# A hybrid attention and recurrence layer: other orders round the fourth head pair, a fifth buffer for raw FFN weights, another cut of the last row

## The chip, the cores and the metric

The kernel runs on one core of one Trainium2 chip. The metric is the device time of one execution in microseconds (us); lower is better. The engines are PE (TensorE), DVE (VectorE), ACT (ScalarE), POOL (GpSimd) and SP (SyncE, which here only starts transfers).

## The reference

One decoder layer over 16 meta tokens and 1024 tokens of width 1024, all in float32:

```python
u = rmsnorm(h, g_pre_mix)
q, k, v, xr, yr = split(u @ w_in)               # 512, 128, 128, 512, 512 columns
attn = sliding_window_attention(q, k, v, sinks) # 8 heads of 64, 2 kv heads, window 128
xr = causal_depthwise_conv(xr, conv_w, conv_b)  # 4 taps
hr = rg_lru(xr, w_a, b_a, w_x, b_x, lam)        # gates, then a scan along the tokens
rec = gelu(yr) * hr
h = h + rmsnorm(concat([attn, rec]) @ w_out, g_post_mix)
h = h + rmsnorm(square(relu(rmsnorm(h, g_pre_ffn) @ w_ff1)) @ w_ff2, g_post_ffn)
```

The attention sees a window of 128 keys, and each head has a sink that takes part in the softmax. The meta tokens are dropped from the output.

## The kernel before, in words

Every float32 operand of a product is split into a high and a low part. ACT writes the high (lines 96 and 117) and DVE the low (lines 99 and 118). `mm3` (lines 125, 128 and 129) issues three matmuls for a product: high by high, high by low, low by high. `behind(name, ...)` lets an instruction stand after another one in the schedule, without a semaphore of its own. The rest of the order comes from a scheduler that works through the program by priorities and by the buffers of the pools.

PSUM has four pools of two banks each: `acc`, `s`, `pt` and `o`. SBUF has pools of rotating buffers by tag, among them `raw` (2 buffers, weights as they come from memory), `e` (2), `d` (4) and `ws` (4, split weights).

The stages, in order of time:

1. Norm, transposition, and the projections to k, v, the first q and the first x.
2. Attention in four head pairs (`j` from 0 to 3). A pair has two halves, and a half two block pairs. For each block pair PE makes scores (lines 592 to 600), DVE adds the mask and takes the row maximum (line 616), ACT takes the exponential (line 82), POOL adds the sums of the parts (line 632), DVE divides (line 633), PE transposes (line 644), ACT and DVE split, POOL masks the diagonals (line 648), and PE multiplies with the values (`av`, line 658). ACT and DVE take the result out (lines 671 and 672). Between these PE has the projections of the later q and x blocks and of y0 to y3 as filling, each in pieces of 256 to 512 columns that use the two `acc` banks in turn. A q piece leaves its bank by `split_scaled`, two highs and two lows; an x piece by an ACT copy (line 460); a y piece by a DVE copy (line 715).
3. The gates of the recurrence (line 800): matmuls that use 64 of the 128 rows, in groups between the pieces of y1 to y3. Then decay, square root and scan on ACT and DVE.
4. The product with `w_out`, its norm, and the first FFN product.
5. The second FFN product as seven block products (`PLAN`), each in eight steps. `fetch_2` loads a step's raw weights three steps ahead, `prep_2` combines two raw blocks where the product needs their sum or difference (`combine`, line 1022) and splits them, `step_mm` multiplies. The raw weights alternate between the two `raw` and the two `e` buffers.
6. The rows of the output: `finish_late` adds the last block product, squares, scales, takes the root, and writes each row of 128 tokens in two halves, one from the SP queue and one from the ACT queue (lines 1418 and 1421). The last row of tokens has its last product in two parts of 256 columns.

The tiles that the change touches: `km` and `vm` hold the keys and values of the meta tokens, `mask` the window's mask. In the kernel before they are three constant tiles, which hold their space to the end.

Of the kernel before, what the change touches and what calls it, by code (L numbers as in the profile page):

```python
# [9 lines left out]
F32 = mybir.dt.float32  # L10
# [27 lines left out]
def hybrid_layer(  # L38
# [15 lines left out]

    bufs = {"raw": 2, "ws": 4, "a": 16, "b": 17, "c": 8, "d": 4, "e": 2}
    uid = [0]
# [200 lines left out]
    def project(w, pieces, sink, begun=None):  # L257
        wh, wl = w
        for t0, n in pieces:
            acc = bank("acc")  # L260
            for kc in range(KC):
                uh, ul = u[kc]
                ins = mm3(
                    acc[:, :n], (wh[:, kc, :], wl[:, kc, :]),
                    (uh[:, t0 : t0 + n], ul[:, t0 : t0 + n]),
                    kc == 0, kc == KC - 1,
                )
                if kc == 1 and begun is not None:
                    begun.append(ins)
            sink(acc[:, :n], t0, n)  # L270
# [167 lines left out]
    def sink_v(acc, t0, n):  # L438
        if t0 == 0:
            nc.scalar.copy(vmt[:, META], acc[:, 0:NMETA])  # L440
        nc.scalar.copy(vt[:, t0 : t0 + n], acc)

    def new_q():
# [65 lines left out]
    for c in range(NLRU):  # L509
# [6 lines left out]

    mask = const.tile([P, 256], F32, name="mask")
    nc.gpsimd.memset(mask, 0.0)
    nc.gpsimd.affine_select(
        out=mask[:, 0:P], in_=mask[:, 0:P], pattern=[[1, P]], compare_op=ALU.is_gt,  # L520
        fill=NEG, base=0, channel_multiplier=-1,
    )
    nc.gpsimd.affine_select(
        out=mask[:, P:256], in_=mask[:, P:256], pattern=[[-1, P]],
        compare_op=ALU.is_ge, fill=NEG, base=0, channel_multiplier=1,
# [53 lines left out]
    def scores(j, half, q):  # L579

        g, pairs = j // 2, []
        for bp in range(2):
# [8 lines left out]
            for h in range(2):  # L591
# [21 lines left out]
                for i in range(2):  # L613
# [23 lines left out]
    def attend(j, half, pairs):  # L637
        g = j // 2
        o_ = slot("e", [P, 512])
        for bp, sn in enumerate(pairs):  # L640
# [15 lines left out]
            def av(v, oc, n, pc, first, last):  # L656
                for k, m in enumerate((mhv, mlv)):
                    nc.tensor.matmul(  # L658
                        po[:, :, oc : oc + n], v, m[:, :, pc : pc + n],
                        start=first and k == 0, stop=last and k == 1,  # L660
                        skip_group_check=True,
                    )

# [46 lines left out]
    def fill_y(c):  # L710
        def run(w):
            y = slot("b" if c == 1 else "d", [P, T])

            def sink(acc, t0, n):
                nc.vector.tensor_copy(y[:, t0 - NMETA : t0 - NMETA + n], acc)

            begun[c] = []
            project(w, REAL2, sink, begun[c])
            ys[c] = y
# [69 lines left out]
    def gates(c):  # L789
# [3 lines left out]
        for t0, n in ((0, 348), (348, 348), (696, 344)):  # L793
# [498 lines left out]
    ]  # L1292

    def fetch_2(n):
        i, q = steps[n]
        if i == 6:
            r = slot(("raw", "e")[n % 2], [P, 2, 512])
            nc.sync.dma_start(r, w2_sum[q])
            return [r]
        wx = PLAN[i][1]  # L1300
        tags = (("raw", "e"), ("e", "raw"))[n % 2]
        raws = []
        for (a, b), tag in zip(wx[:2], tags):
# [34 lines left out]
    for n, p in enumerate(third):  # L1338
# [3 lines left out]
        if n + 2 < 16:  # L1342
            raw_c[third[n + 2]] = fetch_c(third[n + 2])
        if n >= 13:
            raw_2[n - 13] = fetch_2(n - 13)
        if n + 1 < 16:
# [53 lines left out]
    def finish_late(j, y, parts):  # L1400
# [15 lines left out]
        nc.vector.reciprocal(rs, root)  # L1416
        for c, eng in zip(COLS[::-1], (nc.sync, nc.scalar)):
            held.append(nc.vector.scalar_tensor_tensor(
# [105 lines left out]
```

## Time and profile before

| | |
|---|---|
| median of 3 runs | 955.91 us (955.73 to 956.14) |
| profiled execution, its own time | 955.25 us |
| its span | 953.5 us |
| PE busy | 942.0 us, 99% |
| DVE busy | 682.4 us, 72% |
| ACT busy | 498.3 us, 52% |
| POOL busy | 152.7 us, 16% |
| transfers | 140.76 MB, 148 GB/s over the span |

The 1.75 us between the span and the execution's own time lie outside what the profile's rows show. The chain that ended last runs for 88% of the span on PE, for 7% on DVE and for 2% on ACT. A row of the timeline gives start, duration, engine, line, operation, output and inputs; what stands in brackets at its end is the time that the engine stood idle ahead of it, and what released it. Matmuls overlap, so the pace of PE is read from start to start: about 0.23 us for 512 columns and 0.12 us for 256.

### The profile page before, as it was taken

What the parts mean: (1) busy time and instruction counts of PE and PEld (TensorE: products, weight loads), DVE (VectorE), ACT (ScalarE), POOL (GpSimd) and SP (SyncE); (2) the same over time, 40 slices, a digit from 0 to 9 for tenths busy, and PEclk for the clock granted to TensorE, in tenths of its full rate; (3) what the DMA queues carried; (4) which work ended last, traced back from release to release, by engine and by line L of the source; (5) the groups of instructions that cost most, each with busy time, mean ns of one, the idle gap of its engine ahead of it and who ended that gap; (6) DMA issues with size and microseconds to landing.
All of it is one profiled execution on the core that took longest, in us unless ns stands there. A gap on an engine that the chain in (4) does not pass through costs nothing.

```text
span 953.5 us, 12448 instructions
## 1 busy us (share of the span) xinstructions
PE 942.0 (99%) x4677; PEld 785.7 (82%) x4677; DVE 682.4 (72%) x968; ACT 498.3 (52%) x822; POOL 152.7 (16%) x196
## 2 busy tenths in 40 slices
PE   9999999999999999999999999999999999999997
PEld 8999998878788877888888878888888888888886
DVE  6679999777966886665755566567567676779884
ACT  7556676468355564443655565664433343445451
POOL 2115666500021100000111001100111100003020
PEclk9999999999999999999999999999999999999999
DMA  8121101203145457485646457644678865656422
GB/s 293 49 56 34 45 2 34 67 17 117 42 166 192 153 181 238 158 284 177 218 160 216 157 177 217 226 153 109 171 179 188 208 218 185 185 190 155 116 84 89
DMA packets 85629, 140.76 MB, mean 148 GB/s; under 512 B 5785, under 2 KB 48937, under 8 KB 85569
## 3 DMA queue, kind: packets, MB, share of 16 engines
q1 hardware_dynamic: 75104, 108.51, 36.1%
q0 software_dynamic: 9600, 29.36, 11.7%
q10 hardware_dynamic: 864, 2.10, 0.6%
q8 instruction: 37, 0.61, 0.3%
q14 instruction: 24, 0.19, 0.1%
HBM read 115.70 MB, written 23.07 MB: 146 GB/s over the span
## 4 chain that ended last, share of the span: by engine, by line
PE 88%; DVE 7%; ACT 2%; issue 1%; DMA 1%; POOL 1%; DVEq 0%; SPq 0%; ACTq 0%; POOLq 0%
PE ps_acc L125 10%; PE ps_acc L128 10%; PE ps_acc L129 10%; PE ps_pt L128 6%; PE ps_pt L129 6%; PE ps_pt L125 6%; PE ps_s L125 6%; PE ps_s L129 6%; PE ps_s L128 6%; PE ps_o L125 5%; PE ps_o L128 5%; PE ps_o L129 5%; DVE c L852 1%; PE ps_o L658 1%; PE ps_o L996 1%
## 5 line engine op out<-in xcount | busy, mean ns | idle before, releaser
L96 ACT CAST ws<-raw 128x1024 fp32r<-128x1024 f32 (+1 forms) x70 | 71.8, 1025 | 118.9 <-PE ps_o L128 45.8
L99 DVE TENSOR_TENSOR ws<-raw,ws 128x1024 fp32r<-128x1024 f32 (+1 forms) x71 | 85.4, 1203 | 45.5 <-ACT ws L96 45.5
L125 PE MATMUL ps_acc<-a,ws 128*128 128x256 f32 (+2 forms) x256 | 85.5, 334 | 1.1 <-ACT d L460 1.0
L129 PE MATMUL ps_acc<-a,ws 128*128 128x256 f32 (+2 forms) x256 | 85.0, 333 | 0.0
L128 PE MATMUL ps_acc<-a,ws 128*128 128x256 f32 (+2 forms) x256 | 85.0, 332 | 0.0
L99 DVE TENSOR_TENSOR b<-b,b 128x1024 fp32r<-128x1024 f32 (+2 forms) x48 | 57.6, 1199 | 25.5 <-PE ps_o L128 19.8
L96 ACT CAST ws<-e 128x1024 fp32r<-128x1024 f32 x42 | 44.0, 1047 | 57.0 <-PE ps_o L128 31.4
L96 ACT CAST b<-b 128x1024 fp32r<-128x1024 f32 (+2 forms) x48 | 49.5, 1030 | 38.8 <-DVE b L1022 36.4
L99 DVE TENSOR_TENSOR ws<-e,ws 128x1024 fp32r<-128x1024 f32 x42 | 51.3, 1222 | 20.0 <-ACT ws L96 20.0
L648 POOL TENSOR_SCALAR_AFFINE_SELECT c<-c 128x512 fp32r<-128x512 f32 x64 | 55.8, 893 | 26.8 <-ACT c L96 20.6
L125 PEld LDWEIGHTS ps_acc<-a,ws 128*128 128x128 f32 x256 | 48.2, 188 | 6.4 <-ACT d L460 1.2
L129 PEld LDWEIGHTS ps_acc<-a,ws 128*128 128x128 f32 x256 | 48.2, 188 | 5.1 <-issue 0.2
L178 POOL TENSOR_TENSOR rs<-ms,half_pow 128x1 f32<-128x1 f32 x26 | 19.3, 749 | 205.9 <-DVE ms L174 204.7
L128 PEld LDWEIGHTS ps_acc<-a,ws 128*128 128x128 f32 x256 | 48.1, 188 | 4.6 <-issue 0.4
L125 PE MATMUL ps_acc<-ws,b 128*128 128x512 f32 (+1 forms) x120 | 46.3, 385 | 0.0
L129 PE MATMUL ps_acc<-ws,b 128*128 128x512 f32 (+1 forms) x120 | 46.2, 385 | 0.0
L128 PE MATMUL ps_acc<-ws,b 128*128 128x512 f32 (+1 forms) x120 | 46.1, 384 | 0.0
L125 PE MATMUL ps_pt<-ws,b 128*128 128x512 f32 x112 | 44.2, 394 | 0.0
L128 PE MATMUL ps_pt<-ws,b 128*128 128x512 f32 x112 | 44.1, 393 | 0.0
L129 PE MATMUL ps_pt<-ws,b 128*128 128x512 f32 x112 | 43.9, 392 | 0.0
L125 PE MATMUL ps_s<-ws,b 128*128 128x512 f32 x110 | 43.4, 395 | 0.0
L129 PE MATMUL ps_s<-ws,b 128*128 128x512 f32 x110 | 43.2, 393 | 0.0
(429 smaller groups left out, 2720.9 us busy)
## 6 DMA issues: line engine op xcount, KB each, us to landing
raw<-in_w_ff_dram SPq DMA_DIRECT2D x58, 512.0 KB, 4.4
e<-in_w_ff_dram SPq DMA_DIRECT2D x42, 512.0 KB, 4.1
raw<-in_w_in_dram SPq DMA_DIRECT2D x12, 512.0 KB, 5.1
d<-in_w_ff_dram SPq DMA_DIRECT2D x12, 512.0 KB, 4.2
s_dram<-d POOLq DMA_DIRECT2D x12, 512.0 KB, 4.4
e<-in_w_ff_dram POOLq DMA_DIRECT2D x10, 512.0 KB, 5.8
raw<-in_w_ff_dram POOLq DMA_DIRECT2D x10, 512.0 KB, 5.8
c<-in_x_dram SPq DMA_DIRECT2D x8, 512.0 KB, 8.9
```

Of the source, the lines that this page charges most:

```text
L96: nc.scalar.copy(hi, src)
L99: low = nc.vector.tensor_tensor(lo, src, f32(hi), op=ALU.subtract).ins
L125: ins = nc.tensor.matmul(dst, lh, rh, start=start, stop=False, skip_group_check=True).ins
L128: nc.tensor.matmul(dst, lh, rl, start=False, stop=False, skip_group_check=True)
L129: last_mm[0] = nc.tensor.matmul(dst, ll, rh, start=False, stop=stop, skip_group_check=True).ins.name
L178: last_pow[0] = nc.gpsimd.tensor_tensor(rs[:n], ms[:n], half_pow[:n], op=ALU.pow).ins.name
L648: nc.gpsimd.affine_select(out=m[:, :, side, :], in_=f32(m)[:, :, 1, :], pattern=[[0, 4], [-sign, P]], compare_op=op, fill=0.0, base=0, cha ...
L658: nc.tensor.matmul(po[:, :, oc : oc + n], v, m[:, :, pc : pc + n], start=first and k == 0, stop=last and k == 1, skip_group_check=True,)
L852: return nc.vector.tensor_tensor_scan(r, a, gi, 0.0, op0=ALU.mult, op1=ALU.add).ins
L996: nc.tensor.transpose(pt[:, i, :], xn[:, kc * P : (kc + 1) * P], ident)
```

## The change

Six edits go together.

- `km`, `vm` and `mask` become parts of one tile with a tag of its own, `m`. After the attention this space is a fifth buffer for raw weights of the second FFN product. `place` gives each load the buffer that comes free earliest, `in_turn` keeps the loads on SP in program order, loads start four steps ahead instead of three, and a combination of two raw blocks stands behind the last split's low part.
- In the fourth pair the first exponential stands behind the second q3 piece's last high (ACT), and the first row maximum behind its last low (DVE).
- The `av` matmuls of the last block pair stand behind the third k-chunk of y1's first piece. The third token chunk of the first gates stands behind the third k-chunk of y1's second piece (before: the second k-chunk of the first piece).
- The copies of y0 are made by ACT instead of DVE.
- In the last row but one the two halves of the output are released one at a time, each behind a scaling of the last row's two parts.
- The last row's output is cut into 768 columns (SP queue) and 256 columns (ACT queue), instead of 512 and 512.

```diff
-    km = const.tile([P, 2, 2, P], F32R, name="km")
-    vm = const.tile([P, 2, P], F32R, name="vm")
+    both = slot("m", [P, 4, 2, P], F32R)
+    km, vm = both[:, 0:2], both[:, 2]
...
-    mask = const.tile([P, 256], F32, name="mask")
+    mask = f32(both[:, 3].rearrange("p a b -> p (a b)"))
...
-                split_scaled(q[h][r, c], q[h][o, c], acc[r], HD ** -0.5)
+                q_made[:] = split_scaled(q[h][r, c], q[h][o, c], acc[r], HD ** -0.5)
...
-                    lut(
+                    power = lut(
                         sn[:, k, :], sn[:, k, :], AF.Exp, scale=-1.0,
...
+                    if (j, half, bp, k) == (3, 0, 0, 0):
+                        behind(q_made[0].name, power)
+                        behind(q_made[1].name, top)
...
+                    if (j, half, bp) == (NPAIR - 1, 1, 1):
+                        behind(begun[1][2].name, ins)
...
-                nc.vector.tensor_copy(y[:, t0 - NMETA : t0 - NMETA + n], acc)
+                copy = nc.scalar.copy if c == 0 else nc.vector.tensor_copy
+                copy(y[:, t0 - NMETA : t0 - NMETA + n], acc)
...
             if (c, t0) == (0, 696):
-                behind(ins.name, begun[1][1])
+                behind(ins.name, begun[1][KC + 2])
...
+    free = [(-5, "m"), (-4, "e"), (-3, "raw"), (-2, "e"), (-1, "raw")]
+    def place(until):
+        tag = min(free)[1]
+        free.remove(min(free))
+        free.append((until, tag))
+        return tag
+    turn = []
+    def in_turn(ins):
+        if turn:
+            behind(turn[-1], ins)
+        turn.append(ins.name)
...
-            r = slot(tag, [P, 2, 512])
-            nc.sync.dma_start(r, w2v[q, a, b])
+            r = slot(place(n if raws else n + 0.5), [P, 2, 512])
+            in_turn(nc.sync.dma_start(r, w2v[q, a, b]).ins)
...
-            combine(raws[0], raws[0], raws[1], wx[2])
+            behind(mark[0], combine(raws[0], raws[0], raws[1], wx[2]))
...
-            behind(last, *held)
-            held.clear()
             part = squares(y[k], acc[:, c], k)
-            combine(o[:, c], acc[:, c], gffn_b[:, c], ALU.mult)
+            scaled = combine(o[:, c], acc[:, c], gffn_b[:, c], ALU.mult)
+            if len(parts) == 1:
+                behind(last, *held)
+                held.clear()
+            else:
+                behind(scaled.name, held.pop(0))
...
-        for c, eng in zip(COLS[::-1], (nc.sync, nc.scalar)):
+        cut = 256 if j == 3 else 512
+        for c, eng in zip((slice(cut, D), slice(0, cut)), (nc.sync, nc.scalar)):
...
-        if n + 3 < len(steps):
-            raw_2[n + 3] = fetch_2(n + 3)
+        if n + 4 < len(steps):
+            raw_2[n + 4] = fetch_2(n + 4)
```

How the instructions move is shown at three places. Numbers behind the names tell tiles apart, and the same tile has a number that is smaller by one to three in the changed kernel. The lines of the attention move by two to eight.

The first place is ACT where the last q3 piece leaves its bank (L117, `ps_acc_1814`) and the fourth pair's softmax starts (L82). In the kernel before:

```order
L82 ACTIVATE c_2121,den<-c_2121,negm 128x257 x2
L671 COPY e_2236<-ps_o_2274 64x256
L82 ACTIVATE c_2151,den<-c_2151,negm 128x257 x2
L117 ACTIVATE b_1784<-ps_acc_1814 64x512
L671 COPY e_2236<-ps_o_2250 64x256
L671 COPY e_2236<-ps_o_2274 64x256
L460 COPY d_1952<-ps_acc_1953 128x272
L82 ACTIVATE c_2151,den<-c_2151,negm 128x257 x2
```

The same place on ACT in the changed kernel, where the piece is `ps_acc_1812` and line 678 stands for line 671:

```order
L678 COPY e_2234<-ps_o_2272 64x256
L117 ACTIVATE b_1782<-ps_acc_1812 64x512
L678 COPY e_2234<-ps_o_2248 64x256
L678 COPY e_2234<-ps_o_2272 64x256
L82 ACTIVATE c_2119,den<-c_2119,negm 128x257
L462 COPY d_1950<-ps_acc_1951 128x272
L82 ACTIVATE c_2119,den<-c_2119,negm 128x257 x3
L82 ACTIVATE c_2149,den<-c_2149,negm 128x257 x2
```

The second high of the q3 piece now stands ahead of every exponential of the pair, and the copy of x3's first piece (L460, now L462) stands behind one exponential instead of at least four.

The second place is PE at the last values (L658), two output banks `ps_o_2522` and `ps_o_2546`, and then y1's first piece in `ps_acc_2346`. In the kernel before:

```order
L658 MATMUL ps_o_2522<-c_2510,b_278 128x2x128
L658 MATMUL ps_o_2546<-c_2533,b_278 128x512
L658 MATMUL ps_o_2546<-c_2534,b_278 128x512
L658 MATMUL ps_o_2546<-c_2533,b_278 128x2x128
L658 MATMUL ps_o_2546<-c_2534,b_278 128x2x128
L658 MATMUL ps_o_2546<-c_2533,b_278 128x2x128
L658 MATMUL ps_o_2546<-c_2534,b_278 128x2x128
L125 MATMUL ps_acc_2346<-a_93,ws_2179 128x512
```

The same place on PE in the changed kernel, where line 663 stands for line 658 and the names are `ps_o_2544` and `ps_acc_2344`:

```order
L663 MATMUL ps_o_2520<-c_2508,b_277 128x2x128
L125 MATMUL ps_acc_2344<-a_93,ws_2177 128x512
L128 MATMUL ps_acc_2344<-a_94,ws_2177 128x512
L129 MATMUL ps_acc_2344<-a_93,ws_2178 128x512
L125 MATMUL ps_acc_2344<-a_95,ws_2177 128x512
L128 MATMUL ps_acc_2344<-a_96,ws_2177 128x512
L129 MATMUL ps_acc_2344<-a_95,ws_2178 128x512
L125 MATMUL ps_acc_2344<-a_97,ws_2177 128x512
L663 MATMUL ps_o_2544<-c_2531,b_277 128x512
L128 MATMUL ps_acc_2344<-a_98,ws_2177 128x512
L129 MATMUL ps_acc_2344<-a_97,ws_2178 128x512
L125 MATMUL ps_acc_2344<-a_99,ws_2177 128x512
```

The six matmuls of the last bank no longer follow the other six at once: seven matmuls of y1 stand ahead of the first, and four more ahead of the other five.

The third place is PE in the gates (L800), where y2's second piece in `ps_acc_2482` is interrupted. In the kernel before a group of six, after an earlier group of twelve of the same token chunks:

```order
L128 MATMUL ps_acc_2482<-a_98,ws_2341 128x512
L800 MATMUL ps_pt_2678<-b_2609,b_2067 128x344
L800 MATMUL ps_pt_2678<-b_2610,b_2067 128x344
L800 MATMUL ps_pt_2678<-b_2609,b_2067 128x344
L800 MATMUL ps_o_2679<-b_2609,b_2067 128x344
L800 MATMUL ps_o_2679<-b_2610,b_2067 128x344
L800 MATMUL ps_o_2679<-b_2609,b_2067 128x344
L129 MATMUL ps_acc_2482<-a_97,ws_2342 128x512
```

The same gates on PE in the changed kernel, where line 808 stands for line 800 and the piece is `ps_acc_2480`. The twelve rows are the start of one group of 18:

```order
L128 MATMUL ps_acc_2480<-a_102,ws_2339 128x512
L808 MATMUL ps_s_2656<-b_2607,b_2065 128x348
L808 MATMUL ps_pt_2657<-b_2607,b_2065 128x348
L808 MATMUL ps_s_2656<-b_2608,b_2065 128x348
L808 MATMUL ps_pt_2657<-b_2608,b_2065 128x348
L808 MATMUL ps_s_2656<-b_2607,b_2065 128x348
L808 MATMUL ps_pt_2657<-b_2607,b_2065 128x348
L808 MATMUL ps_o_2666<-b_2607,b_2065 128x348
L808 MATMUL ps_s_2667<-b_2607,b_2065 128x348
L808 MATMUL ps_o_2666<-b_2608,b_2065 128x348
L808 MATMUL ps_s_2667<-b_2608,b_2065 128x348
```

Over the whole kernel PE has the gates in groups of 18, 18, 12, 6, 3 and 15 before, and in groups of 6, 12, 18, 18 and 18 now.

More of the change, by code (lines that the diff above doesn't have):

```diff
@@ L53, in hybrid_layer @@
     dpool = ctx.enter_context(tc.tile_pool(name="dpool", bufs=1, space=DRAM))
-    bufs = {"raw": 2, "ws": 4, "a": 16, "b": 17, "c": 8, "d": 4, "e": 2}
+    bufs = {"raw": 2, "m": 1, "ws": 4, "a": 16, "b": 17, "c": 8, "d": 4, "e": 2}
     uid = [0]
@@ L267, in project @@
                 )
-                if kc == 1 and begun is not None:
+                if begun is not None:
                     begun.append(ins)
@@ L515, in hybrid_layer @@
     nc.vector.tensor_scalar(nsink, nsink, -1.0, None, op0=ALU.mult)
-    mask = const.tile([P, 256], F32, name="mask")
+    mask = f32(both[:, 3].rearrange("p a b -> p (a b)"))
     nc.gpsimd.memset(mask, 0.0)
     nc.gpsimd.affine_select(
-        out=mask[:, 0:P], in_=mask[:, 0:P], pattern=[[1, P]], compare_op=ALU.is_gt,
+        out=mask[:, 0:P].bitcast(F32R), in_=mask[:, 0:P], pattern=[[1, P]], compare_op=ALU.is_gt,
         fill=NEG, base=0, channel_multiplier=-1,
@@ L523, in hybrid_layer @@
     nc.gpsimd.affine_select(
-        out=mask[:, P:256], in_=mask[:, P:256], pattern=[[-1, P]],
+        out=mask[:, P:256].bitcast(F32R), in_=mask[:, P:256], pattern=[[-1, P]],
         compare_op=ALU.is_ge, fill=NEG, base=0, channel_multiplier=1,
@@ L657, in av @@
                 for k, m in enumerate((mhv, mlv)):
-                    nc.tensor.matmul(
+                    ins = nc.tensor.matmul(
                         po[:, :, oc : oc + n], v, m[:, :, pc : pc + n],
@@ L1296, in fetch_2 @@
         if i == 6:
-            r = slot(("raw", "e")[n % 2], [P, 2, 512])
-            nc.sync.dma_start(r, w2_sum[q])
+            r = slot(place(n + 0.5), [P, 2, 512])
+            in_turn(nc.sync.dma_start(r, w2_sum[q]).ins)
             return [r]
         wx = PLAN[i][1]
-        tags = (("raw", "e"), ("e", "raw"))[n % 2]
         raws = []
-        for (a, b), tag in zip(wx[:2], tags):
+        for a, b in wx[:2]:
             if len(wx) == 3 and wx[2] is ADD and raws and q % 3 < 2:
```

7 lines of the change are left out of this document (4 added, 3 removed).

## The prediction

> **What bounds the kernel now.** I read the engines of the page first, then the waits of PE, then the stretches of time, then the rows round each wait.
>
> ```profile
> PE 942.0 (99%) x4677; PEld 785.7 (82%) x4677; DVE 682.4 (72%) x968; ACT 498.3 (52%) x822; POOL 152.7 (16%) x196
> ```
>
> PE is busy for 942.0 of the 953.5 us of the span. The change removes no matmul, so it can only win where PE waits or changes its mode, and behind PE's last matmul. The waits of PE between 150 and 222 us, and two stretches with the busy time of the engines in the order PE, PEld, DVE, ACT, POOL:
>
> ```profile
> PE ps_acc L125 <- ACT d L460: 1.0, 1, 1.0
> PE ps_o L658 <- POOL c L648: 0.9, 1, 0.9
> PE ps_acc L125 <- DVE b L715: 0.2, 1, 0.2
> ```
>
> ```profile
> 150.00:222.00 72.00, 69.95 (x415) 58.36 (x414) 58.38 (x96) 44.21 (x94) 20.58 (x21) 1.00 0.15 45
> 636.00:940.00 304.00, 304.00 (x1347) 248.54 (x1346) 222.21 (x212) 133.22 (x159) 29.84 (x24) 1.00 0.58 158
> ```
>
> The end of attention and the gates hold 72.00 - 69.95 = 2.05 us in which PE stands, in three waits. The second FFN product holds none (304.00 of 304.00, at granted clock 1.00). So the larger edits of the diff, the fifth buffer and the earlier loads, have nothing to win there: a load that comes earlier than it must is worth nothing. The gain has to come from the orders round the fourth pair.
>
> **The q3 piece: 0.2 us won.** PE, ACT and DVE where x3's second piece waits for a bank of `acc`:
>
> ```profile
> 156.19 0.28 PE L600 MATMUL ps_s<-b,b 128*128 128x256 f32 x1
> 157.41 0.39 PE L125 MATMUL ps_acc<-a,ws 128*128 128x256 f32 x1 [0.95 <-ACT d L460]
> ```
>
> ```profile
> 155.70 0.59 ACT L117 ACTIVATE b<-ps_acc 64x512 fp32r<-64x512 f32 x1
> ```
>
> ```profile
> 152.93 1.22 DVE L99 TENSOR_TENSOR ws<-raw,ws 128x1024 fp32r<-128x1024 f32 x1
> ...
> 157.95 0.69 DVE L118 SCALAR_TENSOR_TENSOR b<-ps_acc,b 64x512 fp32r<-64x512 f32 x1
> ```
>
> From the score at 156.19 to the piece at 157.41 PE takes 1.22 us; a step takes 0.12, so the stand is 1.10. Before, the piece takes the bank of x3's first piece. In the new order it takes the bank of q3's second piece, which is free once its last low is made (157.95 + 0.69 = 158.64 before). That low is moved ahead of the row maxima. On DVE it stands behind the low of a weight, which ends at 152.93 + 1.22 = 154.15. Then come the first low (0.69, to 154.84), the second high on ACT (0.59, to 155.43) and the second low (0.69, to 156.12). PE arrives earlier than before: eight score matmuls of 0.12 that stood ahead of the piece now stand behind its start, so it arrives at 156.31 - 0.96 = 155.35. It stands until 156.12, with some 0.1 between engines for 0.9. The net is 1.10 - 0.9 = 0.2 won. The bounds are 0.6 (the three steps overlap at their ends, and PE arrives later) and 0 (two output copies that stand between the lows on DVE hold the second back). The softmax of the pair's first block pair ends up to 5 us later, since its exponentials stand behind this piece. Its transposes are later in PE's order too, and stay behind the division in it.
>
> **The last values: 1.0 us won.** PE at the last `av`, and POOL's last selects:
>
> ```profile
> 182.11 1.33 PE L658 MATMUL ps_o<-c,b 128*128 128x512 f32 x7
> 184.35 0.98 PE L658 MATMUL ps_o<-c,b 128*128 128x512 f32 x5 [0.91 <-POOL c L648]
> ```
>
> ```profile
> 181.04 3.26 POOL L648 TENSOR_SCALAR_AFFINE_SELECT c<-c 128x512 fp32r<-128x512 f32 x3 [0.81 <-DVE c L99]
> ```
>
> ```profile
> 183.83 1.29 DVE L715 COPY d<-ps_acc 128x512 f32<-128x512 f32 x2
> ```
>
> ```profile
> 181.40 0.62 ACT L96 CAST b<-e 128x512 fp32r<-128x512 f32 x1 [1.81 <-DVE e L672]
> ```
>
> The last select ends at 181.04 + 3.26 = 184.30, and PE stands 0.91 for it, and 0.1 more to get going. Now seven matmuls of y1 with 0.23 each stand ahead of the last bank (1.6) and four more ahead of its low part (0.9). PE starts the twelve 0.2 earlier by the term above, at 181.9; six take 1.1, so the low part is needed at 181.9 + 1.1 + 1.6 + 0.2 + 0.9 = 185.7, 1.4 after the select's end. The wait goes, 1.0 won. This needs y1's bank of `acc` by 183.0. DVE's copies of y0 at 183.83 would free it too late; that is what the copies on ACT are for. ACT stood idle for 1.81 ahead of 181.40, room for a copy of that size (0.69 on DVE), so they cost nothing; without this cover the wait would come back at y1's bank.
>
> **The bank of y1: 0.4 us won.** PE and DVE at y2's first matmul:
>
> ```profile
> 191.14 0.39 PE L129 MATMUL ps_acc<-a,ws 128*128 128x512 f32 x1
> 191.72 0.47 PE L125 MATMUL ps_acc<-a,ws 128*128 128x512 f32 x1 [0.19 <-DVE b L715]
> ```
>
> ```profile
> 190.88 0.69 DVE L715 COPY b<-ps_acc 128x512 f32<-128x512 f32 x1 [1.73 <-PE ps_acc L129]
> ```
>
> Three matmuls of y1's second piece stood between the first piece's end and y2, which needs its bank. The copy takes 0.69 and starts 0.2 after the piece. PE went from 191.14 to 191.72 in 0.58 instead of 0.23, so 0.35 were lost. Now six matmuls stand there, 1.4 us, and the copy is done 0.5 before that. The wait goes. DVE was idle for 1.73 ahead of this copy, so nothing is queued there that could delay it.
>
> **One group of gates less: 0.4 us won.** PE round a group of six gate matmuls:
>
> ```profile
> 208.82 0.39 PE L128 MATMUL ps_acc<-a,ws 128*128 128x512 f32 x1
> 209.14 0.42 PE L800 MATMUL ps_pt<-b,b 64*128 64x344 f32 x1
> ...
> 209.82 0.50 PE L129 MATMUL ps_acc<-a,ws 128*128 128x512 f32 x1
> 210.16 0.39 PE L125 MATMUL ps_acc<-a,ws 128*128 128x512 f32 x1
> ```
>
> Into the group PE takes 0.32 instead of 0.23, and out of it 0.34 instead of 0.23. Between, the six matmuls, which run in pairs, take 0.68 from 209.14 to 209.82; at the pace of the 512 columns (0.23), three times 344 columns are 0.46. That is 0.09 + 0.11 + 0.22 = 0.4 for a group, waits apart. Six groups become five.
>
> So the product with `w_out` starts 0.2 + 1.0 + 0.35 + 0.4 = 2.0 earlier. Against this I set 0.1 for new short waits: y copies by DVE stand close to the use of their bank at two places, and one of 0 to 0.8 can come out of the new order of the `w_out` weights among the gates' activations.
>
> **Behind the gates: 0.3 us won.** ACT, DVE and PE in the scan:
>
> ```profile
> 226.91 1.05 ACT L96 CAST a<-d 128x1024 fp32r<-128x1024 f32 x1 [0.86 <-DMA d<-in_w_out_dram]
> ```
>
> ```profile
> 231.53 1.24 DVE L842 SCALAR_TENSOR_TENSOR c<-b,c 128x1040 f32<-128x1040 f32 x1 [1.72 <-ACT c L82]
> ```
>
> ```profile
> 261.47 0.39 PE L125 MATMUL ps_pt<-a,b 128*128 128x512 f32 x1
> 261.92 0.50 PE L128 MATMUL ps_pt<-a,b 128*128 128x512 f32 x1
> ```
>
> DVE works without a gap from 231.53 to the operand that PE stands for at 261.92, 0.45 instead of 0.23 a step and 0.1 behind it: 0.3 lost. The chain starts behind ACT's roots, which stand behind this cast and its wait. In the new order the cast is ahead of the last decay, so DVE starts 1.05 + 0.86 earlier, and 2.0 more with PE's gates. PE itself comes 2.0 earlier, so some 1.9 are left to cover 0.3.
>
> **The second FFN product: 0.** The nearest rows, DVE with a combination and a low, and PE with the matmul that uses the low:
>
> ```profile
> 721.57 1.22 DVE L1022 TENSOR_TENSOR raw<-raw,e 128x1024 f32<-128x1024 f32 x1
> 722.70 1.22 DVE L99 TENSOR_TENSOR ws<-raw,ws 128x1024 fp32r<-128x1024 f32 x1
> ```
>
> ```profile
> 725.67 0.40 PE L128 MATMUL ps_acc<-ws,b 128*128 128x512 f32 x1
> ```
>
> The low is there at 723.92 and used at 725.67: 1.75 spare. `in_turn` queues a load behind the earlier loads on SP, and the combination behind the last split on DVE, one instruction of 1.22. Both fit in the spare time, so I take nothing. The first load into the new buffer now stands on SP ahead of the `w_out` weights; these wait for a later low on DVE anyway.
>
> **The tail: 0.** DVE in the last row, ACT's last issue, and the transfers from 949 to 953.5 in 40 slices:
>
> ```profile
> 947.56 0.41 DVE L1022 TENSOR_TENSOR a<-ps_acc,a 128x256 f32<-128x256 f32 x1
> ...
> 949.08 1.41 DVE L1418 SCALAR_TENSOR_TENSOR a<-a,rs,d 128x512 f32<-128x512 f32 x2
> ```
>
> ```profile
> 950.52 0.34 ACTq L1421 DMA_DIRECT2D out_dram<-a  x1
> ```
>
> ```profile
> GB/s 0 0 0 0 0 0 0 0 0 73 0 0 0 0 18 346 328 382 437 346 346 346 419 364 400 400 364 164 0 0 0 0 0 0 0 0 0 0 0 0
> ```
>
> With one half of the row before released, not both, ahead of the last add, that add (947.56) can start up to 0.4 earlier, but then the other half (0.7) stands ahead of the reciprocal, and 0.2 is left. The first piece then takes 768 columns instead of 512, 0.3 longer, and its store starts at 949.1 - 0.2 + 1.05 instead of 949.1 + 0.7: 0.1 later. The 512 KB of the last row flow in one stretch of 13 slices at 346 to 437 GB/s, so the end follows the first store and not the second. I take 0, from -0.4 (the end follows the last issue, 0.2 earlier, and a smaller piece) to +0.2. The Trainium skill, DMA: Bandwidth & Descriptors, section "Issuing engines are not separate DMA queues", says that transfers of different issuing engines share the same 16 engines and interleave. By that rule another cut over the two queues moves the bytes no faster, and the tail is worth 0; the trace's unbroken stretch agrees.
>
> **The sum.** 0.2 + 1.0 + 0.35 + 0.4 - 0.1 + 0.3 + 0 + 0 = 2.15 us. Against the profiled execution (span 953.5, with 1.75 outside it 955.25) this gives 953.1. The median of the runs, 955.91, lies 0.66 above that execution, so I forecast 953.1 + 0.7 = 953.8 as the median.
>
> **Rivals.** *The removed waits come back at a new place (no change).* POOL's selects are not of one length:
>
> ```profile
> L648 POOL TENSOR_SCALAR_AFFINE_SELECT c<-c x64: 631/638/3191, 69.4 to 183.3; 128x512 fp32r<-128x512 f32 x64
> ```
>
> Minimum, median and maximum are 631, 638 and 3191 ns; the last three took 3.26 together while DVE was at work. One that is 2.55 longer eats the 1.4 that the last values have in hand, and PE stands for 1.15 again; a `w_out` copy that is 0.8 late makes it 1.95, and 0.2 are left of the gain: 955.8. With the select alone it is 955.0. For it: all of the fourth pair's softmax is later and closer to other DVE work. Against it: the last selects are behind work that the new order hardly moves. The Trainium skill, SBUF — State Buffer, section "SBUF: two separate sides", says that VectorE instructions with two SBUF inputs and GpSimd instructions that read SBUF lock each other out for a whole instruction. By that rule the long selects recur wherever such work meets them; the lengths in the row agree. I give this 0.25.
>
> *The second FFN product gets waits (slower).* The combination now stands behind the last split. If at a step two instructions of 1.22 stand ahead of it and of the low where one stood, or SP's order holds a load back as long, the low is 2.44 - 1.75 = 0.69 late, and PE stands at each such step. 16 steps subtract two raw blocks on DVE; all of them would cost 11.0, a kernel of 964.8, and half of them 5.5, 959.3. It decides from (1.9 + 2.1)/0.69, 6 steps, on that the kernel is slower by over 0.2%. Against it: DVE is idle for 23 of each 100 us there (222.21 of 304.00 busy). I give it 0.14.
>
> **How the numbers follow.** 0.2% is 1.9 us, about what a measurement of this kernel can tell from no change, so faster is below 954.0. My forecast has 0.61: its own range runs from 952.9 (q3's wait shrinks by 0.6 instead of 0.2, the tail wins 0.4, no new wait) to 954.9 (q3 wins nothing, one new wait of 0.8, the tail 0.2 longer). As 953.8 is close to 954.0, 0.51 of it lie below and 0.10 above. The first rival ends within 0.2% with 0.22 and below with 0.03. The second is slower, 0.14. Faster 0.54, same 0.32, slower 0.14. The range takes in the first rival and the light end of the second, four steps late by 0.69 (953.8 + 2.8): up to 956.6. Below I leave 0.4 beyond the forecast's own range, for waits that the rows join to others: 952.5.
>
> **What would show it right or wrong.** Right: in the changed kernel PE waits 0.7 to 1.0 for DVE's L118 near 155, no longer for L648 and the y1 copy, the gates come in five groups, the first matmul of the `w_out` product starts 2.0 earlier, the stretch of the second FFN product stays full, and from PE's last matmul to the end the time is the same within 0.3. Wrong: a new wait of PE between 155 and 226, or any in the last 300 us.

## The result, and the profile after

The changed kernel takes 954.19 us in the median of 22 runs (953.59 to 955.67), the kernel before 955.99 in 22 runs beside them (955.23 to 958.21). The ratio is 0.9980, with an interval of 0.9974 to 0.9986: 1.8 us or 0.19% faster, and 0.4 us above the 953.8 forecast. The prediction counts less than 0.2% as the same, and gave "faster" the larger chance (0.54); the median lies just inside "same", and the interval reaches to both sides of that bound. The profiled execution takes 953.82 us (span 952.1), against 955.25 (953.5) before.

The engines, the waits of PE between 150 and 226 us, and the two stretches, in the same views as before:

```profile
PE 941.1 (99%) x4677; PEld 785.6 (83%) x4677; DVE 681.4 (72%) x966; ACT 499.8 (52%) x824; POOL 154.3 (16%) x196
```

```profile
PE ps_o L663 <- POOL c L653: 1.0, 2, 0.5
```

```profile
150.00:222.00 72.00, 71.02 (x425) 59.64 (x424) 58.30 (x97) 48.13 (x102) 21.83 (x22) 1.00 0.19 60
636.00:940.00 304.00, 304.00 (x1346) 248.56 (x1345) 220.72 (x213) 131.34 (x158) 29.86 (x24) 1.00 0.57 158
```

PE stood for 2.05 us in the first stretch before and stands for 0.98 now. Two of the three waits are gone, the one for L460 and the one for the y1 copy, but POOL's selects (now L653) are waited for twice instead of once. Here they are on PE's timeline:

```profile
150.13 1.33 PE L663 MATMUL ps_o<-c,b 128*128 128x512 f32 x7
151.96 0.98 PE L663 MATMUL ps_o<-c,b 128*128 128x512 f32 x5 [0.50 <-POOL c L653]
...
156.12 0.29 PE L129 MATMUL ps_acc<-a,ws 128*128 128x272 f32 x1
156.25 0.28 PE L125 MATMUL ps_acc<-a,ws 128*128 128x256 f32 x1
...
181.77 0.39 PE L663 MATMUL ps_o<-c,b 128*128 128x512 f32 x1
182.64 0.98 PE L663 MATMUL ps_o<-c,b 128*128 128x512 f32 x5 [0.48 <-POOL c L653]
183.45 0.40 PE L125 MATMUL ps_acc<-a,ws 128*128 128x512 f32 x1
...
191.09 0.39 PE L129 MATMUL ps_acc<-a,ws 128*128 128x512 f32 x1
191.32 0.39 PE L125 MATMUL ps_acc<-a,ws 128*128 128x512 f32 x1
```

At 156.25 x3's second piece starts without a wait, and at 191.32 y2 starts without one. But at 151.96 PE stands for the third pair's values, where it came through before, and at 182.64 for the low part of the bank ahead of the last one.

PE's last matmul in the kernel before (first fence), and in the changed kernel (second):

```profile
946.81 0.28 PE L129 MATMUL ps_acc<-a,b 128*128 128x256 f32 x1
```

```profile
944.42 0.28 PE L129 MATMUL ps_acc<-a,b 128*128 128x256 f32 x1
```

PE is done 2.39 earlier, but the span is only 1.4 shorter: from the start of the last matmul to the end, the tail, it takes 6.74 before (946.81 to 953.55) and 7.70 now (944.42 to 952.12). To see where each part comes from, I laid the two profiles' matmuls side by side, one matmul against the same one; a minus is time won:

| place | forecast | measured |
|---|---|---|
| the first 11 us | 0 | +0.14 |
| q3 piece, 150 to 158 us | -0.2 | -0.44 (a stand of 1.11 gone, one of 0.67 new) |
| last values, 182 us | -1.0 | -0.43 (1.07 became 0.64) |
| y1's bank, 191 us | -0.35 | -0.35 |
| gates | -0.4 | -0.92 |
| short new waits | +0.1 | 0 |
| behind the gates, 261 us | -0.3 | -0.32 |
| second FFN product | 0 | 0 |
| other places before it | 0 | -0.07 |
| tail | 0 | +0.96 |
| sum | -2.15 | -1.43 |

### The profile page after: what moved, and what is told of

Its sections match the earlier page's. It is cut to its first block, busy times and chain, and to the rows that moved or that the text cites. A ratio compares the mean times of both kernels' runs of the same rounds, so it can differ in the third digit from the quotient of the medians.

```text
span 952.1 us, 12444 instructions
## 1 busy us (share of the span) xinstructions
PE 941.1 (99%) x4677; PEld 785.6 (83%) x4677; DVE 681.4 (72%) x966; ACT 499.8 (52%) x824; POOL 154.3 (16%) x196
## 4 chain that ended last, share of the span: by engine, by line
PE 94%; DVE 2%; POOL 2%; ACT 1%; DMA 0%; issue 0%; SPq 0%; DVEq 0%; ACTq 0%; POOLq 0%
PE ps_acc L125 11%; PE ps_acc L128 11%; PE ps_acc L129 11%; PE ps_pt L125 7%; PE ps_pt L129 7%; PE ps_pt L128 6%; PE ps_s L125 6%; PE ps_s L129 6%; PE ps_s L128 6%; PE ps_o L128 5%; PE ps_o L125 5%; PE ps_o L129 5%; POOL c L653 1%; PE ps_o L663 1%; PE ps_o L1004 1%; PE ps_s L602 1%
## 5 line engine op out<-in xcount | busy, mean ns | idle before, releaser
L96 ACT CAST ws<-raw 128x1024 fp32r<-128x1024 f32 (+1 forms) x64 | 65.4, 1022 | 100.7 <-PE ps_o L128 47.1
L99 DVE TENSOR_TENSOR ws<-raw,ws 128x1024 fp32r<-128x1024 f32 (+1 forms) x65 | 78.2, 1203 | 38.0 <-ACT ws L96 37.9
L653 POOL TENSOR_SCALAR_AFFINE_SELECT c<-c 128x512 fp32r<-128x512 f32 x64 | 56.2, 901 | 24.0 <-ACT c L96 20.3
```

The lines of the kernel that those rows point to most:

```text
L96: nc.scalar.copy(hi, src)
L99: low = nc.vector.tensor_tensor(lo, src, f32(hi), op=ALU.subtract).ins
L653: nc.gpsimd.affine_select(out=m[:, :, side, :], in_=f32(m)[:, :, 1, :], pattern=[[0, 4], [-sign, P]], compare_op=op, fill=0.0, base=0, cha ...
```

## The experiments

Three questions were open: what makes the tail longer, which edits carry the gain, and whether the two waits for POOL can go.

### The tail: are its own edits to blame?

In the changed kernel I put back the old tail (both halves of the row before released ahead of the last add, a cut of 512 and 512):

```diff
+            behind(last, *held)
+            held.clear()
             part = squares(y[k], acc[:, c], k)
...
-        for c, eng in zip((slice(cut, D), slice(0, cut)), (nc.sync, nc.scalar)):
+        for c, eng in zip(COLS[::-1], (nc.sync, nc.scalar)):
```

> The changed kernel with the tail of before: both halves of row 2 released together ahead of the last add, the last row cut 512 and 512. All else as changed. Theory A (the new tail itself costs time: from PE's last matmul to the end the trace shows 7.7 us instead of 6.7): the tail goes back to 6.7 and the kernel is about 1.0 faster than the changed one, 953.2, or 2.8 under before. Rival B (the 1.0 is how the last transfers of one execution happened to land): the kernel stays within 0.3 of the changed one, 954.2, 1.8 under before. Theory of the prediction (tail worth 0 to within 0.4): 953.8 to 954.6.

Two more put back only one half of this. With the release one at a time, but the old cut:

> The changed kernel with the last row cut 512 and 512 again, but the halves of row 2 still released one after the other. If the late release is what costs (row 2's second half is stored 1 us later, and its 256 KB run into the last row's stores), the tail stays at about 7.7 and the time near 954.2. If the cut costs (the store of 128 KB, with 1 KB a row, lands 3.3 us after its issue instead of 2.1), the tail falls to 6.7 minus the 0.3 that the reciprocal comes earlier: 6.4, and 952.9 in all.

With the new cut, but both halves released together:

> The changed kernel with both halves of row 2 released together again, but the last row still cut 768 and 256. If the cut costs, the tail stays at 7.7 or goes to 8.0 (the reciprocal is later by 0.3), the time near 954.2 to 954.5. If the late release costs, the tail falls to 6.7 to 7.0, and the time to about 953.2 to 953.5.

The medians are 953.95, 954.18 and 954.25, all within 0.25 us of the changed kernel's (ratios 0.9982, 0.9986 and 0.9986, each with some 0.0009 to both sides). So the clean comparison is the tail itself. The old tail's code takes 7.69 in this kernel, not 6.74: the loss is not due to the edits of the tail. Release alone has 7.41, cut alone 7.99, both together 7.70. So the release wins 0.28, the cut costs 0.30, and the two come to nothing, on top of a loss that is common to all four.

To see if such a loss comes and goes from one execution to the next, I ran the kernel before once more as one of the kernels:

> The kernel before once more, with nothing changed. It measures what two sets of runs of one kernel differ by, and takes a second profile of the kernel before. Theory V (the length of the first 11 us and of the landing of the last store vary from execution to execution): PE's last matmul to the end is 7.4 to 7.8 us here and not the 6.7 of the first profile, with each engine's instruction behind the last matmul at the same distance to within 0.05. Rival (the 6.7 belongs to the kernel before): 6.7 again. The median is within 0.5 of the other runs of before under either.

Its tail is 6.73, as in the first profile, and its median 956.17 (ratio 1.0001, 0.9993 to 1.0010). The changed kernel, run again further below, has 7.74. The tail belongs to the kernel, not to the execution.

What differs is a transfer that none of the kernel's instructions issues: one packet of 8 KB on a queue that the profile calls "instruction". The transfers of the changed kernel from 949.7 to 950.2 (the view books a packet's bytes where the packet starts, hence the 655; this one takes 0.31 us):

```profile
GB/s 83 82 82 0 82 0 0 0 655 0 0 0 0 0 0 0 0 0 0 0 0 0 0 0 0 0 0 0 0 0 0 0 82 0 0 0 82 0 0 0
...
q10 hardware_dynamic: 12, 0.01, 4.6%
q14 instruction: 1, 0.01, 3.9%
```

And from 946.6 to 952.1, to be held against the row from 949 to 953.5 of the kernel before:

```profile
GB/s 0 0 0 0 328 417 343 417 343 60 0 0 313 447 402 380 402 424 380 254 320 350 120 60 0 15 7 0 0 0 0 0 0 0 0 0 0 0 0 0
```

Before, the stores flow at full rate and stop at once. Now the rate falls to 15 and 7 GB/s for the last slices: single packets of the last store, which land late, while all else is done. Sorted by the code of the tail, with the time behind the last matmul at which that packet moves (windows of 0.5 us):

| code of the tail | kernel | packet at | tail, us |
|---|---|---|---|
| old | before; before again; gates only; gates and loads | 3.0 to 3.5 | 6.74; 6.73; 6.74; 6.73 |
| old | old tail | 5.0 to 5.5 | 7.69 |
| release, old cut | values later twice, in both executions | 7.0 to 7.5 | 6.44; 6.46 |
| release, old cut | values later once; release only | 4.5 to 5.5 | 7.29; 7.41 |
| release, new cut | without the q3 order | 7.5 to 8.0 | 7.00 |
| release, new cut | changed; changed again; old loads | 5.0 to 5.5 | 7.70; 7.74; 7.75 |
| new cut only | cut only | 5.5 to 6.0 | 7.99 |

With the same code the tail is 0.7 to 1.0 longer wherever the packet falls 4.5 to 6.0 us behind the last matmul, into the last store's data, and never elsewhere. SP waits at the end for all stores to land. Here is that wait for one and the same code of the tail, first in the kernel before, then in the changed kernel with the old tail:

```profile
SPq L1519 <- DMA out_dram<-a: 1.9, 2, 1.3
```

```profile
SPq L1541 <- DMA out_dram<-a: 2.9, 2, 1.6
```

The traces also hold the landings of the last store one by one: it lands in 16 parts. In the first of these two profiles all 16 come 5.59 to 5.77 us behind the last matmul. In the second, 15 come at 5.61 to 5.78 and the last one at 6.72. The packet moves from 5.36 to 5.67, and the next packet of the store that starts behind it starts at 5.67. It is so in every profile: in the seven with a long tail one part of 16 is 0.85 to 0.99 behind the others, and the span ends 2.32 to 2.35 behind the packet's start; in the seven others the 16 parts lie within 0.2. So one part of the last store, which lands behind the packet, makes the tail long. No run moved the packet alone, so that the packet is what holds this part back is the reading that fits all fourteen profiles, and not shown by itself. Which engine's code it carries also stays open.

### Where the gain comes from

From the kernel before I made one with nothing but the new place of the gates' third chunk:

```diff
-                if kc == 1 and begun is not None:
+                if begun is not None:
...
-                behind(ins.name, begun[1][1])
+                behind(ins.name, begun[1][KC + 2])
```

> The kernel before with one edit: the third token chunk of the first gates behind the third k-chunk of y1's second piece. On PE the gates then come in four groups of 18, where there were groups of 18, 18, 12, 6, 3 and 15. Theory G (a split costs what the rows of the two traces give: 0.4 for 12 and 6, 0.9 for 3 and 15): the gates take 7.3 us of PE instead of 8.6, PE ends 1.3 earlier than in the kernel before, about 954.6 as a median. The prediction's price (0.4 a split): 0.8 earlier, 955.1. The waits near 156, 183 and 191 stay.

And the same with the fifth buffer and the earlier loads as well:

> As the run before it, with the fifth buffer, the four steps of lead and the order of the loads for the second FFN product added; PE's order is the same. Prediction's theory (worth 0, PE does not wait there): same median within 0.3. Theory I (the loads are late in some executions only: with four buffers DVE and ACT wait 16 to 30 us for raw weights in that stretch, and a low came 0.05 ahead of its use): DVE's and ACT's waits for raw weights fall to 9 to 12 together, the least lead of a low stays at 1.75, and the median is 0.3 to 0.8 lower.

Beside them the changed kernel again:

> The changed kernel once more, for a second profile and a median beside the run that follows. 954.0 to 954.5; PE stands near 151 and near 182 for 0.65 each, as in the first profile. If the landing of the last store varies by execution, the time from PE's last matmul to the end is anything from 6.7 to 7.8; if it belongs to the kernel, 7.7.

In the gates alone the matmuls of the gates run in four groups of 18. They give 954.36 (ratio 0.9986, 0.9977 to 0.9995), gates and loads 953.84 (0.9980, 0.9971 to 0.9988), the whole change 954.04 (0.9982, 0.9973 to 0.9990). So the gates' edit carries most of the gain and the loads perhaps the rest, and the orders of the q3 piece and the last values, the copies of y0 and the tail come to nothing together in the medians. On PE the orders do win something: from 20 to 270 us, one matmul against the same one, the changed kernel gains 2.41 on the kernel before and the gates alone 1.72. The tail, 7.70 against 6.74, takes that 0.7 back. The waits of PE in the profile of gates alone, between 150 and 226, show why so little code does so much:

```profile
PE ps_acc L125 <- ACT d L460: 1.0, 1, 1.0
PE ps_o L658 <- POOL c L648: 0.9, 1, 0.9
```

The two long waits are still there, but that for the y1 copy is gone, since the gates no longer cut up y1. The split of 3 and 15 matmuls is gone as well, which was the dearest. PE at the group of 3 in the kernel before:

```profile
213.84 0.40 PE L129 MATMUL ps_acc<-a,ws 128*128 128x512 f32 x1
214.17 0.74 PE L800 MATMUL ps_s<-b,b 64*128 64x348 f32 x3
214.84 0.50 PE L129 MATMUL ps_acc<-a,ws 128*128 128x512 f32 x1
```

The way into the three matmuls and through them takes 1.00, from 213.84 to 214.84; 0.23 of it is the step of the 512 columns. Measured over whole groups, the way out included, 18 gate matmuls cost 1.83, 12 cost 1.36, 6 cost 0.87, 3 cost 0.87 and 15 cost 1.84. Three cost as much as six, and 15 as much as 18: three matmuls of a group of 18 have lost the partner that they run beside. Cutting 18 into 12 and 6 thus costs 0.40, as forecast, but into 3 and 15 it costs 0.88.

The loads, in turn, were tried from the other side, the changed kernel with the loads of before:

> The changed kernel with the loads of the second FFN product as before: two raw and two e buffers in turn, loads three steps ahead, no order among the loads, the combination free. The fifth buffer stays unused. Prediction's theory (PE has no wait there, so these edits are worth nothing): the stretch of the second FFN product stays without a wait and the time within 0.3 of the changed kernel, 954.2. Rival (the order of the loads is needed by the rest, or it wins something in another place): slower by 0.5 or more, with waits of PE in the last 300 us.

It has 954.77 (0.9990, 0.9981 to 0.9999), 0.6 above the changed kernel. The step from gates alone to gates and loads is 0.52. Neither difference is clear of the scatter of the runs (by resampling them, 95% of the values lie between -0.1 and 1.5 for the step, and between -0.3 and 1.3 for the old loads). Both point the same way, and the profiles say what the buffer buys. The waits of DVE and ACT for raw weights from 640 to 930 us, in gates alone:

```profile
ACT ws L96 <- DMA e<-in_w_ff_dram: 9.2, 3, 3.6
ACT ws L96 <- DMA raw<-in_w_ff_dram: 5.6, 2, 3.0
DVE raw L1022 <- DMA e<-in_w_ff_dram: 5.0, 1, 5.0
DVE raw L1022 <- DMA raw<-in_w_ff_dram: 4.2, 5, 1.6
DVE e L1022 <- DMA raw<-in_w_ff_dram: 3.6, 2, 3.0
DVE e L1022 <- DMA e<-in_w_ff_dram: 1.7, 4, 0.8
```

and in gates and loads:

```profile
DVE m L1025 <- DMA e<-in_w_ff_dram: 3.6, 1, 3.6
DVE e L1025 <- DMA raw<-in_w_ff_dram: 2.9, 2, 2.3
DVE raw L1025 <- DMA raw<-in_w_ff_dram: 1.6, 2, 0.9
...
DVE e L1025 <- DMA m<-in_w_ff_dram: 0.5, 1, 0.5
```

29.3 us of waits become 8.6, and none is left on ACT. In both profiles PE does not stand for them, since DVE and ACT work ahead. In the second profile of the kernel before it does; DVE, and PE, which uses its low:

```profile
757.76 1.23 DVE L1023 TENSOR_TENSOR raw<-raw,e 128x1024 f32<-128x1024 f32 x1 [3.34 <-DMA e<-in_w_ff_dram]
758.90 1.22 DVE L100 TENSOR_TENSOR ws<-raw,ws 128x1024 fp32r<-128x1024 f32 x1
```

```profile
759.30 0.39 PE L126 MATMUL ps_o<-ws,b 128*128 128x512 f32 x1
760.18 0.50 PE L129 MATMUL ps_acc<-ws,b 128*128 128x512 f32 x1 [0.48 <-DVE ws L100]
```

DVE stood 3.34 for a load, and PE lost 0.73 by it, against the same matmuls of the first profile. The shortest lead of a low on its matmul is 1.65 in that first profile, 0.06 here (760.12 to 760.18), and 0.41 in the changed kernel with the old loads; with five buffers it is 1.75 in all five profiles compared, and with four it was 1.75 too in the gates alone. So four buffers are late in some executions only.

### Can the waits for POOL go?

First the q3 piece's order, taken out of the changed kernel:

```diff
-                    if (j, half, bp, k) == (3, 0, 0, 0):
-                        behind(q_made[0].name, power)
-                        behind(q_made[1].name, top)
```

> The changed kernel without the two orders of the fourth pair's first exponential and row maximum behind the q3 piece. Prediction's theory (the order moves the q3 piece out of its bank earlier): PE stands near 156 for an ACT copy again, 1.1, and not near 151; PE is 0.4 later than in the changed kernel at the start of y0 and from there on. Rival (the order does nothing that the other edits do not): same waits as the changed kernel.

The waits of PE from 145 to 262 us in its profile:

```profile
PE ps_acc L125 <- ACT d L462: 1.0, 1, 1.0
PE ps_acc L125 <- ACT d L720: 0.2, 1, 0.2
```

The old wait for x3's copy is back, and both waits for POOL are gone. The 0.2 is y1's wait for its bank, which ACT's copy of y0 still holds. Its one run takes 952.92; the clearer reading is PE's place from 20 to 270 us, one matmul against the same one: it wins 2.66 on the kernel before, against 2.39 to 2.50 in six profiles with the order. So the order removed a wait of 1.0 and made two, and by this one profile it costs some 0.2.

Then the values of the block pair before the last, moved behind the second k-chunk of y1's first piece as well (this kernel and the next two have the old cut of 512 and 512):

```diff
+                    if (j, half, bp) == (NPAIR - 1, 1, 0):
+                        behind(begun[1][1].name, ins)
```

> The changed kernel with the values of the block pair before the last one ordered behind y1's second k-chunk as well (so four matmuls of y1 stand ahead of them), and the last row cut 512 and 512. Theory S (the 0.64 that PE still stands near 182 is the wait for POOL's select of the low part, and 0.93 of y1 work covers it): no wait of PE for POOL near 182, and PE's last matmul 0.6 earlier than in the changed kernel, at 943.8; the time 0.6 to 0.9 under it, 953.3 to 953.6. Rival (PE then catches another input of the same stage): a new wait of 0.3 to 0.7 between 182 and 226, and no gain.

```profile
PE ps_acc L125 <- ACT d L725: 0.8, 1, 0.8
PE ps_o L663 <- POOL c L653: 0.5, 1, 0.5
```

The 0.5 is the stand at the third pair's values, as in the changed kernel. The wait at 182 is no longer for POOL but, 0.8 long, for ACT's copy of y0, which holds y1's bank of `acc`. The median is 955.05 (0.9987, 0.9978 to 0.9996): no gain. Last, the same with the third pair's values treated likewise, behind pieces of x3:

```diff
+                    if (j, half) == (2, 1) and ("x", 3) in begun:
+                        behind(begun["x", 3][1 + 2 * bp].name, ins)
```

> As the run before it, and the values of the third pair's second half behind the second and fourth k-chunk of x3's first piece, so that four and seven more matmuls of x3 stand ahead of them. Theory S: the 0.67 that PE stands near 151 falls to 0.2 or less, PE's last matmul comes 0.3 to 0.6 earlier again, at 943.2 to 943.5. Rival: the output copies of these values come later, hold the second low of q3 back on DVE, and PE stands for x3's second piece near 155 again, for 0.3 to 0.7: no gain over the run before.

> Once more the kernel that has the values of the third and of the fourth pair behind matmuls of x3 and y1, and the last row cut 512 and 512. By its trace it spares the two waits of 0.65 and so 1.3 to 1.5 of the changed kernel: 952.5 to 953.0 by that alone. If its first median, 951.4, holds, it has something more: the end, 6.4 instead of 7.7 in the traces.

The medians are 951.41 (0.9951, 0.9939 to 0.9964) and, in the second run, 951.27 (0.9953, 0.9939 to 0.9966): 4.4 us faster than before and 2.8 faster than the change, and its profile has 72.00 of 72.00 us of PE:

```profile
150.00:222.00 72.00, 72.00 (x430) 60.93 (x429) 59.63 (x99) 49.89 (x103) 21.80 (x22) 1.00 0.19 60
```

By the same count as above, PE wins 3.86 on the kernel before by 270 us, 1.45 more than the changed kernel. The device of the change, used at two more places, brings that. Most of the rest of the 2.8 is the tail, 6.46 instead of 7.70: 0.3 of it is the old cut, and the other 0.9 goes with the packet, which here falls behind the last store. Nothing in the edit aims at that, so it is luck.

## Why the prediction was right, and where only its sum was

**Right, with the size.** The y1 bank (0.35), the stretch behind the gates (0.32 against 0.3), and PE's start on the product with `w_out`: 227.38 before, 225.44 after, 1.94 earlier where 2.0 was forecast. The second FFN product holds no wait in this profile, as said, and the gates come in five groups. The start on `w_out` is near by luck in part: the last values won 0.57 less than forecast, the gates 0.52 and the q3 piece 0.24 more, and the first 11 us were 0.14 longer. Of the signs that the prediction named, three failed: PE does not wait for L118 near 155, it still waits for a select at 182, and the tail is not the same within 0.3.

**The q3 piece: right mechanism, wrong opponent.** The step that failed had PE standing until DVE's second low at 156.12. The low ended at 155.68 and PE came at 156.25, since x3's own matmuls filled the gap, so the stand went altogether. What I left out is what the moved scores did in front of it: without them PE reached the third pair's values earlier (150.13 against 150.46 before), and stood 0.67 there for a select. The run without the order shows that this, with the one at 182, cost more than was won.

**The last values: mis-sized, 1.0 against 0.43.** I costed the last bank alone, and that one waits for nothing. The bank ahead of it had no matmuls put in front of it. PE reached it 0.34 earlier than before (181.77 against 182.11), and the select that its low part needs came later than before, at 182.58: in the kernel before PE took that part at 182.35 without a wait. POOL in the changed kernel:

```profile
178.24 6.56 POOL L653 TENSOR_SCALAR_AFFINE_SELECT c<-c 128x512 fp32r<-128x512 f32 x7 [0.56 <-DVE c L99]
```

Seven selects in one row take 6.56, 0.94 each against the median of 0.638 shown before; the fifth ends at 182.58. Without the q3 order no wait for POOL is left there, so this term was spoiled by the other one. So the first rival, POOL's long selects, came true in part: two stands of 0.67 and 0.64 where it priced one of 1.15, while the late `w_out` copy that it added did not come. It was not decisive, since the gates gave more than forecast.

**The gates: mis-sized, 0.4 against 0.92.** The step that failed took the cost of the split of 12 and 6 for that of 3 and 15. That odd group stands in the order of the kernel before, and I did not look at its rows.

**The tail: the largest miss, 0 against +0.96, and not by its edits.** The prediction's ends were -0.4 and +0.2. The two edits came out as it had them. The release wins 0.28 where it said 0.2. The cut costs 0.30, and with it the first store is issued 0.27 later and the second no later than without, so the end does follow the first store. Together they are +0.01 with the packet in the way (7.69 to 7.70). Where it is out of the way there is one profile with both, at 7.00 against 6.74; its last store lands 0.04 later than in the kernel before, and the other 0.2 is DVE, which comes late to the last meeting of the engines, behind the landing. The step that failed is the premise that only the kernel's own stores move in the tail, which left its time the same within 0.3. An instruction packet moves there too, and one of the last store's 16 parts lands behind it, 0.9 late. The Trainium skill, DMA: Bandwidth & Descriptors, section "Issuing engines are not separate DMA queues", by which transfers of different engines interleave on the same 16 engines, stood for a tail of 0. For the two edits together the runs agree, with 7.69 and 7.70.

**The fifth buffer: 0 in the profile, some 0.5 in the median.** The step that failed is "a load that comes earlier than it must is worth nothing". It read one execution, in which the loads were in time by 1.65. In the second profile of the same kernel the lead was used up and PE lost 0.73, and insurance against that shows only in a median. Together the misses come to +0.72 in the profile (1.43 won instead of 2.15). The median, with 1.8 won, has 0.4 of it back. That is about what the loads seem to be worth, but that they are the reason is not shown.

The second rival, waits in the second FFN product, is false: the loads are the one part that works against such waits. (By its own figures, 222.21 of 304.00 busy, DVE is idle for 27 of each 100 us there and not for 23, which speaks against this rival all the more.) The forecast's margin of 0.2 us to the bound of "same" was as thin as it looked. That it missed by 0.4 only is luck in part: gains that were not forecast (0.52 at the gates, 0.24 at the q3 piece, 0.4 between profile and median) stand against losses that were not (0.57 at the last values, 0.96 in the tail).

## What to carry to other kernels

When a wait on PE is removed by moving work, ask what PE reaches earlier now: the matmul just behind the moved work may have the next late operand, as at two places here. Price a group of small matmuls by whether each of them has a partner to run beside, not by one measured split. And a tail is measured between the same two events in several builds, since something that no line of the kernel issues may fall into it.

## What the runs showed of the hardware

**Instruction packets move among the data.** One of 8 KB takes 0.31 us. Where it falls into the last store, one of the store's 16 parts lands 0.85 to 0.99 us behind the others, and the tail is 0.7 to 1.0 us longer than with the same code elsewhere. In the runs here its place behind the last matmul changed from kernel to kernel, between 3.2 and 7.6 us, also by edits far from the tail, and by 0.25 at most between two executions of one kernel.

**The first 11 us vary by up to 1.8 us between executions of one kernel.** The first matmuls of the kernel with the values moved twice, in two executions; first the one of 952.75 us, then the one of 951.16:

```profile
1.58 5.06 PE L298 MATMUL ps_acc<-m 128*128 128x512 f32 x11 [1.58 <-POOL m L292]
8.29 2.06 PE L298 MATMUL ps_acc<-m 128*128 128x512 f32 x4
```

```profile
1.58 4.47 PE L299 MATMUL ps_acc<-m 128*128 128x512 f32 x11 [1.58 <-POOL m L293]
7.66 1.18 PE L299 MATMUL ps_acc<-m 128*128 128x512 f32 x4
```

The same four matmuls take 2.06 or 1.18: 0.43 a step against 0.23. The windows view gives a granted clock of 1.00 in both, but it counts time without a clock record as full: the traces' first record, of the full clock, begins at 11.06 us in the first and at 5.22 in the second, just where the steps change. The Trainium skill, TensorE: Matmul & The Clock Gate, section "Part 1: The HAM clock gate (the "warmup" mystery)", says that the window which opens the clock runs freely, so that the moment of the change varies from run to run; the two steps, near one to two, agree with it. A gain of under 2 us is therefore not read from the spans of two profiles, but from one matmul against the same one, behind the start.
